# Units claimed for the first round of the weight stream, routing by logits in all groups, and a first gathering in four parts

## The chip, the cores and the metric

The kernel runs on one core of one Trainium2 chip. The metric is device time in microseconds (us), the median of repeated runs. One execution is recorded by the hardware profiler: its span runs from its first to its last instruction, and its own time is a little longer.

## The reference, cut to what matters

A two-layer block of three branches (state-space scan, sliding window, forgetting attention) is followed by a second block of three branches and a mixture of experts. The change lies in the mixture alone:

```python
t = h.reshape(-1, d)                                  # 256 tokens of 1024, after an rms norm
g_prob = softmax(t @ w_group + b_group)               # 4 groups
g_idx, g_gate = argmax(g_prob), max(g_prob)
e_logits = (t @ w_expert).reshape(-1, 4, 8) + b_expert
e_prob = softmax(e_logits[the token's group])         # 8 experts of that group
top_p, top_i = top_k(e_prob, 2)
top_w = g_gate * top_p / sum(top_p)
for e in range(32):
    hid = silu(t @ w_gate[e]) * (t @ w_up[e])         # 1024 -> 512
    out = out + combine[:, e] * (hid @ w_down[e])     # 512 -> 1024
x = x + out
```

All 32 experts' weights are read, in float32: 3 x 2 MiB each, 201 MB in all.

## The kernel before, in words

**Stages.** Two layers of the first block, then the second block (its last step is the product with `w_out_2`, line 1299), then the mixture, `moe` (from line 1385). Instructions are put in order ahead of time by a scheduler that works by priority with a model of the time; each engine then runs its own list in order. `high_priority` moves instructions forward; `pin` keeps TensorE's products of the mixture in the order in which they are written. A tile gets its buffer when its first writer is scheduled, and gives it back after its last reader.

**The weight stream.** The experts' weights come as 384 pieces of 512 KB (128 x 1024 float32), 24 for each of 16 pairs of experts: 16 pieces of `w_gate_2` and `w_up_2`, then 8 of `w_down_2`. `fetch` (line 1329) issues them on the queue of SyncE (SP) strictly in order of use, and `ring` (line 1313) says into which buffer. `RING` names 35 buffers: 2 `we`, 6 `u`, 4 `wx`, 5 `wraw`, 5 `whi`, 4 `wlo`, 4 `Thi`, 4 `Tlo` and 1 `rowb`. `FIRST` adds 4 more `u` once, so that pieces 35 to 38 (counted from 0) go into extra buffers; from piece 39 on the 35 buffers come round again, each as soon as its old piece has been read. Eight pieces are fetched inside the second block (`ahead`), the others when the buffers of the earlier stages come free.

**Units.** A `unit` (line 270) is one of 16 buffers of 128 x 1024 float32, all named `u`. In the mixture 6 of them belong to the ring, 4 hold x split into two halves (`hk`, `hlk`), 2 the router's weights (until the router's products are done), 2 each round's gathered tokens (`xg`), and 2 each pair's output (`yh`, `yl`) until it is scattered back. In the kernel before, the 4 extra units of `FIRST` are taken when their transfer is scheduled, from what is free then. `unit(True)` claims one at its place in the program by a one-column memset on GpSimd (POOL).

**Router (lines 1410 to 1497).** x is turned by TensorE (`tsplit`), ScalarE (ACT) and VectorE (DVE) write the two halves; ACT also squares x and copies it into `hk`, DVE subtracts into `hlk` (lines 1417 to 1420). Products give the logits, which are turned back (line 1437, tile `tp`) and scaled (line 1439). DVE then takes the first maximum over the groups, picks the logits of the token's group, takes the softmax with ACT, takes two first maxima of 8, and spreads the result over 32 experts (`m32`). Two products give each token's place in its expert's list (`rank`), from which `onehot` makes the matrix of a round of 4 experts.

**Rounds.** A round is 4 experts, 64 places each, in two pairs. `gather` (line 1507) brings tokens to their places, 2 of 8 slices of x at a time: 8 products and an eviction by DVE. `places` turns the one-hot matrix and gathers the weights. `hidden` does the 64 products of a pair with `w_gate_2` and `w_up_2` in 4 parts, `turned` turns the result, `down` does the 32 products with `w_down_2`, and `scatter` adds the outputs of two pairs to x. For the first round all four gathers and `places` come ahead of the first `hidden`; for later ones they stand around `turned`.

Of the kernel before, what the change touches and what calls it, by code (L numbers as in the profile page):

```python
# [25 lines left out]
F32 = mybir.dt.float32  # L26
# [16 lines left out]

FIRST = "u" * 4

# [76 lines left out]
def tile_model(ctx: ExitStack, tc: tile.TileContext, I: dict, out: bass.AP):  # L122
# [15 lines left out]
    def wtile(shape, dt, name, bufs=2):  # L138
        return (scope[0] if name in common else scope[-1]).tile(shape, dt, name=name, bufs=bufs)
# [1161 lines left out]

    extra, turns, last, fetched, slots = [], [0], [], [], []
    flat = lambda w: w.rearrange("p a n -> p (a n)")
# [48 lines left out]

    def first_max(v, n, wts, oh, mx, dst=None):

        V.tensor_reduce(mx, v, axis=AX.X, op=OP.max)
        V.tensor_tensor(oh, v, mx[:, :, None].to_broadcast([128, 2, n]), op=OP.is_equal)
        V.tensor_tensor(oh, oh, wts[:, None, :n].to_broadcast([128, 2, n]), op=OP.mult)
        cm = wtile([128, 2], F32, name="fm_c")
        V.tensor_reduce(cm, oh, axis=AX.X, op=OP.max)
        V.tensor_tensor(oh if dst is None else dst, oh, cm[:, :, None].to_broadcast([128, 2, n]), op=OP.is_equal)  # L1360

# [23 lines left out]
    def moe(router):  # L1385
# [24 lines left out]
        with tc.high_priority(HPR):  # L1410

            for c in range(2):
                for t in range(2):
                    cs = slice(512 * c, 512 * c + 512)
                    tsplit(x[:, t, cs], t, pair[c])
                    sq = wtile([128, 512], F32, name="th")
                    S.activation(sq, x[:, t, cs], AF.Square, accum_out=ss[:, t, c:c + 1])
                    xv, ps_ = x[:, t, cs].rearrange("q (p k) -> q k p", k=8), slice(64 * c, 64 * c + 64)
                    S.copy(hk[t][:, :, ps_], xv)
                    V.tensor_sub(hlk[t][:, :, ps_], xv, hk[t][:, :, ps_].bitcast(F32))  # L1420
            ps = psum.tile([128, 512], F32, name="proj", bufs=3)
            for K in range(8):
# [4 lines left out]
                if K < 7:  # L1427
                    mm(ps[0:36, :256], wrs[:, K, 0:36], xl[:, K % 4, :], False, False)
            lgT = wtile([128, 256], F32, name="lgT", bufs=1)
            S.copy(lgT[0:72], ps[0:72, :256])  # L1430
# [3 lines left out]
            tp = psum.tile([128, 4, 128], F32, name="tp", bufs=2)  # L1434
            lg = wtile([128, 2, 36], F32, name="lg", bufs=1)
            for t in range(2):
# [3 lines left out]
            mx, gate, m0, m1, z = (wtile([128, 2], F32, name=f"r{i}", bufs=1) for i in range(5))  # L1440
            ohg, t4 = R_(4, "ohg"), R_(4, "t4")
            first_max(lg[:, :, 0:4], 4, wts, ohg, mx)
            V.tensor_tensor(t4, lg[:, :, 0:4], b_(mx, 4), op=OP.subtract)
            S.activation(t4, t4, AF.Exp)
            V.tensor_reduce(gate, t4, axis=AX.X, op=OP.add)
            V.reciprocal(gate, gate)
            t32, el, pe, oh0, oh1 = R_(32, "t32"), R_(8, "el"), R_(8, "pe"), R_(8, "oh0"), R_(8, "oh1")
            for t in range(2):
                V.tensor_tensor(t32[:, t].rearrange("p (g e) -> p g e", g=4),
                                lg[:, t, 4:36].rearrange("p (g e) -> p g e", g=4),  # L1450
                                ohg[:, t, :, None].to_broadcast([128, 4, 8]), op=OP.mult)
                V.tensor_reduce(el[:, t], t32[:, t].rearrange("p (g e) -> p e g", g=4), axis=AX.X, op=OP.add)
            V.tensor_reduce(mx, el, axis=AX.X, op=OP.max)
            V.tensor_tensor(pe, el, b_(mx, 8), op=OP.subtract)
            S.activation(pe, pe, AF.Exp)
            V.tensor_reduce(z, pe, axis=AX.X, op=OP.add)
            V.reciprocal(z, z)
            V.tensor_tensor(pe, pe, b_(z, 8), op=OP.mult)
# [4 lines left out]
            member = R_(8, "member")  # L1463
            V.tensor_add(member, oh0, oh1)
            m32 = wtile([128, 2, 32], F32R, name="m32", bufs=1)

            c3 = wtile([128, 2, 16, 3], F32, name="c3", bufs=1)
            comb = c3[:, :, :, 0:2]
            for t in range(2):
                V.tensor_copy(c3[:, t, :, 2:3], rs[:, t:t + 1, None].to_broadcast([128, 16, 1]))  # L1470

            def spread(dst, src):
                for t in range(2):
                    V.tensor_tensor(dst[:, t].rearrange("p (g q) c -> p g q c", g=4),
                                    ohg[:, t, :, None, None].to_broadcast([128, 4, 4, 2]),
                                    src[:, t].rearrange("p (q c) -> p q c", c=2)[:, None].to_broadcast([128, 4, 4, 2]),
                                    op=OP.mult)
# [5 lines left out]
            pcv = pc[:, 0:128].rearrange("p (a e) -> p a e", a=4)  # L1483
            rank, many = R_(32, "rank"), R_(32, "many")
# [4 lines left out]
            V.tensor_add(z, m0, m1)  # L1489
            V.reciprocal(z, z)  # L1490
            V.tensor_mul(z, z, gate)
            V.tensor_mul(m0, m0, z)
            V.tensor_mul(m1, m1, z)
            V.tensor_tensor(oh0, oh0, b_(m0, 8), op=OP.mult)
            V.tensor_tensor(oh1, oh1, b_(m1, 8), op=OP.mult)
            V.tensor_add(oh0, oh0, oh1)
            spread(comb, oh0)

# [19 lines left out]
        def places(q, ohv, xg):  # L1518

            got = []  # L1520
            for a in range(2):
# [14 lines left out]
                got.append((xg, 128 * a, cg, ohT))  # L1536
            return got

        halves64 = (slice(0, CAP), slice(CAP, 2 * CAP))

        def hidden(p, xg, a, cg):
            pg, pu = (psum.tile([128, 512], F32, name="proj", bufs=3) for _ in range(2))
            for i in range(4):
                for ps, nme in ((pg, "w_gate_2"), (pu, "w_up_2")):
                    ws = [piece(nme, 2 * p + a, i) for a in range(2)]
                    for j in range(2):
                        k = 2 * i + j
                        for w, r in zip(ws, halves64):
                            xk = xg[k][0][:, xg[k][1], a + r.start:a + r.stop]
                            pin(T.matmul(ps[r], xk, w[:, 512 * j:512 * j + 512], start=k == 0, stop=k == 7))  # L1550
            hid = wtile([128, 512], F32, name="th")
# [43 lines left out]
        xg, ohv = [], onehot(0)  # L1595
        for k0 in range(0, 8, 2):
            gather(ohv, xg, k0)
        blocks = lambda got: [([(g[0][k // 4], k % 4) for k in range(8)], *g[1:]) for g in got]
        ready, back = blocks(places(0, ohv, xg)), []
        for p in range(16):  # L1600
            own, a, cg, ohT = ready.pop(0)
            more = not ready and p < 15
# [14 lines left out]
            if more:  # L1617
                ready = places(p // 2 + 1, ohv, xg)
                gather(ohv, xg, 4)
                gather(ohv, xg, 6)  # L1620
                ready = blocks(ready)
            back.append((down(p, hT), ohT))
# [111 lines left out]
```

## Time and profile before

| what | us |
|---|---|
| median of 3 runs | 1823.84 |
| lowest and highest run | 1822.07, 1827.51 |
| the profiled execution, its own time | 1828.07 |
| its span | 1826.3 |
| busy in the span: TensorE products / VectorE / ScalarE / GpSimd | 1711.4 / 1029.5 / 708.7 / 316.9 |
| bytes moved | 389.65 MB |

The profile cuts the span into 40 slices of about 45.7 us. In it PE is TensorE's products, PEld its weight loads, DVE VectorE, ACT ScalarE, POOL GpSimd, SP SyncE, whose queue issues the transfers. The last ten slices and a few more are the mixture; there the row of GB/s stands at 409 nearly throughout, and the slice ahead of them has 89.

### The profile page before, as it was taken

How to read it: one execution, taken by the hardware profiler on the slowest of the kernel's cores; microseconds unless marked ns; L12 is line 12 of the kernel's file. 1: busy time of each engine (PE TensorE's matmuls, PEld its weight loads, DVE VectorE, ACT ScalarE, POOL GpSimd, SP SyncE). 2: the span in 40 equal slices, each digit the busy share in tenths (PEclk: the TensorE clock that was granted, in tenths of full speed). 3: DMA queues.
4: the chain of work that ended last, by engine and by line, in shares of the span. 5: the costliest groups of instructions: out<-in, count | busy, mean ns of one | idle time of the engine just before them, and what ended most of it. 6: DMA issues, size and time to landing. Idle time of an engine off the chain costs nothing.

```text
span 1826.3 us, 24145 instructions
## 1 busy us (share of the span) xinstructions
PE 1711.4 (94%) x9005; PEld 1270.2 (70%) x9005; DVE 1029.5 (56%) x1670; ACT 708.7 (39%) x1345; POOL 316.9 (17%) x243
## 2 busy tenths in 40 slices
PE   7999999999999999999998988867799999999998
PEld 6999888888798898888877767755544343434342
DVE  6656657656664486766769998898512121211121
ACT  5556555645444656655546542413310000000000
POOL 1111116110102002311034433463000000000000
PEclk9999999999999999999999998888899999999999
DMA  8645444465466443453755532126729999999997
GB/s 268 197 132 151 133 152 129 137 196 166 145 184 192 133 143 112 133 179 106 239 165 150 152 104 71 48 91 208 252 89 406 409 409 409 409 409 409 409 409 299
DMA packets 186104, 389.65 MB, mean 213 GB/s; under 512 B 28736, under 2 KB 66816, under 8 KB 185984
## 3 DMA queue, kind: packets, MB, share of 16 engines
q1 hardware_dynamic: 185984, 388.08, 62.4%
q8 instruction: 72, 1.18, 0.3%
q14 instruction: 48, 0.39, 0.1%
HBM read 386.98 MB, written 1.05 MB: 212 GB/s over the span
## 4 chain that ended last, share of the span: by engine, by line
PE 62%; DMA 23%; DVE 10%; POOL 2%; issue 2%; ACT 1%; SPq 0%; DVEq 0%; POOLq 0%; ACTq 0%
PE proj L149 46%; PE sc L149 5%; PE pv L149 4%; DMA u<-in_w_up_dram 3%; DMA wraw<-in_w_up_dram 2%; DMA Tlo<-in_w_up_dram 2%; DMA whi<-in_w_up_dram 2%; PE proj L1550 2%; DMA wlo<-in_w_up_dram 2%; DMA Thi<-in_w_up_dram 2%; DMA wx<-in_w_up_dram 2%; DVE wlo L217 2%; PE tp L365 1%; PE sc L1571 1%; DMA wlo<-in_w_down_dram 1%
## 5 line engine op out<-in xcount | busy, mean ns | idle before, releaser
L216 ACT CAST whi<-wraw 128x1024 fp32r<-128x1024 f32 x336 | 351.8, 1051 | 316.9 <-PE proj L149 269.3
L217 DVE TENSOR_TENSOR wlo<-wraw,whi 128x1024 fp32r<-128x1024 f32 (+1 forms) x287 | 374.9, 1309 | 172.1 <-PE proj L149 121.8
L149 PE MATMUL proj<-wlo,Thi 128*128 128x512 f32 (+1 forms) x1056 | 419.4, 397 | 4.7 <-DVE wlo L217 4.6
L149 PE MATMUL proj<-whi,Thi 128*128 128x512 f32 (+1 forms) x1056 | 419.3, 399 | 2.4 <-ACT P L988 1.0
L149 PE MATMUL proj<-whi,Tlo 128*128 128x512 f32 (+1 forms) x1056 | 415.9, 396 | 0.1
L149 PEld LDWEIGHTS proj<-wlo,Thi 128*128 128x128 f32 x1056 | 201.3, 191 | 46.9 <-DVE wlo L217 6.3
L149 PEld LDWEIGHTS proj<-whi,Thi 128*128 128x128 f32 x1056 | 201.5, 191 | 44.8 <-DVE u L1273 1.9
L149 PEld LDWEIGHTS proj<-whi,Tlo 128*128 128x128 f32 x1056 | 201.0, 190 | 41.0 <-DVE Tlo L288 0.7
L217 POOL TENSOR_TENSOR wlo<-wraw,whi 128x1024 fp32r<-128x1024 f32 (+1 forms) x49 | 125.0, 2552 | 440.1 <-PE proj L149 332.9
L149 PE MATMUL proj<-Thi,wlo 128*128 128x256 f32 x576 | 165.3, 289 | 3.7 <-DVE wlo L217 3.7
L149 PE MATMUL proj<-Thi,whi 128*128 128x256 f32 x576 | 164.3, 290 | 2.9 <-ACT Thi L958 1.9
L149 PE MATMUL proj<-Tlo,whi 128*128 128x256 f32 x576 | 164.1, 289 | 0.0
L1553 DVE SCALAR_TENSOR_TENSOR th<-th,cg,proj 128x512 f32<-128x512 f32 x16 | 12.0, 747 | 267.5 <-PE proj L1550 267.5
L149 PEld LDWEIGHTS proj<-Thi,wlo 128*128 128x128 f32 x576 | 112.8, 196 | 4.1 <-DVE wlo L217 3.9
L149 PEld LDWEIGHTS proj<-Thi,whi 128*128 128x128 f32 x576 | 111.8, 195 | 4.5 <-ACT Thi L958 2.4
L149 PE MATMUL sc<-u 128*128 128x256 f32 (+1 forms) x416 | 101.1, 360 | 14.4 <-DVE u L930 14.4
L149 PEld LDWEIGHTS proj<-Tlo,whi 128*128 128x128 f32 x576 | 112.0, 196 | 0.3 <-DVE Tlo L959 0.2
L1552 ACT ACTIVATE th<-proj,cg 128x512 f32<-128x512 f32 x16 | 11.0, 687 | 234.5 <-PE proj L1550 234.5
L149 PEld LDWEIGHTS sc<-u 128*128 128x128 f32 x416 | 70.2, 197 | 22.4 <-issue 14.5
L1575 DVE TENSOR_TENSOR u<-sc,u 128x512 fp32r<-128x512 f32 x32 | 22.1, 692 | 99.8 <-ACT u L1574 99.6
L356 ACT ACTIVATE P<-sc,nm 128x256 f32<-128x256 f32 (+1 forms) x152 | 63.9, 433 | 35.9 <-DVE nm L349 21.8
L1574 ACT CAST u<-sc 128x512 fp32r<-128x512 f32 x32 | 18.8, 586 | 129.2 <-PE sc L1571 129.2
(471 smaller groups left out, 2514.4 us busy)
## 6 DMA issues: line engine op xcount, KB each, us to landing
wraw<-in_w_in_dram SPq DMA_DIRECT2D x236, 512.0 KB, 3.8
wraw<-in_w_proj_dram SPq DMA_DIRECT2D x48, 512.0 KB, 4.2
u<-in_w_up_dram SPq DMA_DIRECT2D x25, 512.0 KB, 10.2
wraw<-in_w_out_dram SPq DMA_DIRECT2D x24, 512.0 KB, 4.2
u<-in_w_gate_dram SPq DMA_DIRECT2D x24, 512.0 KB, 10.2
wraw<-in_w_up_dram SPq DMA_DIRECT2D x21, 512.0 KB, 10.2
whi<-in_w_down_dram SPq DMA_DIRECT2D x21, 512.0 KB, 10.2
u<-in_w_down_dram SPq DMA_DIRECT2D x21, 512.0 KB, 10.2
```

The costliest lines, as they stand in the source:

```text
L149: T.matmul(o, l, r, start=start, stop=stop)
L216: S.copy(hi[:, :, :n], raw[:, :, :n])
L217: (G if share[0] and scount[0] % share[0] == 0 else V).tensor_sub(lo[:, :, :n], raw[:, :, :n], hi[:, :, :n].bitcast(F32))
L356: S.activation(P[:, i * nS:(i + 1) * nS], scv[:, i, :], AF.Exp, bias=nm[:, i:i + 1], accum_out=l_out[:, i:i + 1])
L365: T.transpose(tp[:, j, :], P[:, j * 128:(j + 1) * 128], ident)
L1550: pin(T.matmul(ps[r], xk, w[:, 512 * j:512 * j + 512], start=k == 0, stop=k == 7))
L1552: S.activation(hid, pg, AF.Silu, scale=cg[:, 1:2])
L1553: V.scalar_tensor_tensor(hid, hid, cg[:, 0:1], pu, op0=OP.mult, op1=OP.mult)
L1571: pin(T.matmul(po[c][r], hT[:, k, r], w[:, 512 * c:512 * c + 512], start=k == 0, stop=k == 3))
L1574: S.copy(yh[:, c], po[c])
L1575: V.tensor_sub(yl[:, c], po[c], yh[:, c].bitcast(F32))
```

## The change

Three things. (1) The four extra units are claimed by `unit(True)` after the first `onehot`, and `ring` hands them out; before, each was taken when its transfer was scheduled. (2) The first two experts are chosen among the raw logits in all four groups at once (8 sets of 8 for the two halves of the tokens), and the group's own mask is multiplied in afterwards; the exponentials and the weights are worked out after `rank` (13 instructions on DVE and 2 on ACT, among them the three copies into `c3`), and the copies into `hk` and `hlk` stand after the router's products. (3) The first round's gathering stands inside the first `hidden`: each of its four parts goes ahead of the quarter of the products that reads it, and `places` ahead of the last quarter.

```diff
-FIRST = "u" * 4
+FIRST = 4
@@ ring
-        if n < len(RING + FIRST):
-            w = kinds[(RING + FIRST)[n]]()
-            if n < len(RING):
-                slots.append(w)
+        if n < len(RING):
+            w = kinds[RING[n]]()
+            slots.append(w)
             return w
-        return slots[(n - len(FIRST)) % len(RING)]
+        if n < len(RING) + FIRST:
+            return firsts.pop(0)
+        return slots[(n - FIRST) % len(RING)]
@@ moe, router
-                    S.copy(hk[t][:, :, ps_], xv)
-                    V.tensor_sub(hlk[t][:, :, ps_], xv, hk[t][:, :, ps_].bitcast(F32))
...
             S.copy(lgT[0:72], ps[0:72, :256])
...
+            for c in range(2):
+                for t in range(2):
+                    S.copy(hk[t][:, :, ps_], xv)
+                    V.tensor_sub(hlk[t][:, :, ps_], xv, hk[t][:, :, ps_].bitcast(F32))
...
-            first_max(lg[:, :, 0:4], 4, wts, ohg, mx)
...
-            first_max(pe, 8, wts, oh0, m0)
-            V.scalar_tensor_tensor(el, oh0, -4.0, pe, op0=OP.mult, op1=OP.add)
-            first_max(el, 8, wts, oh1, m1)
+            V.tensor_copy(el, lg[:, :, 4:36])
+            first_max(by8(el), 8, wts, by8(oh0), m0)
+            V.scalar_tensor_tensor(pe, oh0, -3e38, el, op0=OP.mult, op1=OP.add)
+            first_max(by8(pe), 8, wts, by8(oh1), m1)
+            first_max(lg[:, :, 0:4], 4, wts, ohg, mg)
             V.tensor_add(member, oh0, oh1)
-            spread(m32.rearrange("p t (q c) -> p t q c", c=2), member)
+            V.tensor_tensor(by8(m32), by8(member), b8(gexp), op=OP.mult)
...
             V.tensor_tensor(rank, rank, m32.bitcast(F32), op=OP.mult)
...
@@ hidden
             for i in range(4):
+                if prior is not None:
+                    prior(i)
@@ rounds
         xg, ohv = [], onehot(0)
-        for k0 in range(0, 8, 2):
-            gather(ohv, xg, k0)
-        ready, back = blocks(places(0, ohv, xg)), []
+        firsts.extend(unit(True) for _ in range(FIRST))
+        ready, back = [(xg, 0, None)], []
+        def opening(i):
+            gather(ohv, xg, 2 * i)
+            if i == 3:
+                ready[:] = places(0, ohv, xg)
         for p in range(16):
-            hid = hidden(p, own, a, cg)
+            hid = hidden(p, ready, opening if p == 0 else None)
```

## Rows read from the trace of the kernel before

**Rows 1.** Chain that ended last, in order of time: start us, length us, what.
```profile
1331.33 13.91 PE proj L1550 x64
...
1347.56 7.09 PE sc L1571 x32
1354.64 10.32 PE proj L1550 x48
1365.36 4.84 DMA we<-in_w_up_dram
1370.22 10.60 DMA wx<-in_w_down_dram
...
1793.50 10.18 DMA whi<-in_w_up_dram
```

**Rows 2.** Stretches: length, busy by engine, granted clock, DMA share, GB/s.
```profile
1312.00:1329.00 17.00, 9.00 (x40) 8.26 (x40) 9.28 (x56) 0.79 (x3) 0.00 (x0) 0.50 1.02 410
1329.00:1331.00 2.00, 1.78 (x18) 1.69 (x16) 1.31 (x4) 0.37 (x1) 0.00 (x0) 1.00 0.47 186
1331.00:1362.00 31.00, 29.41 (x139) 10.24 (x141) 3.63 (x10) 4.10 (x6) 0.00 (x0) 1.00 0.00 1
1362.00:1372.00 10.00, 8.09 (x30) 2.26 (x26) 0.00 (x0) 0.69 (x1) 0.00 (x0) 1.00 0.75 244
1372.00:1800.00 428.00, 410.70 (x1806) 168.50 (x1806) 79.03 (x152) 38.78 (x69) 0.00 (x0) 1.00 1.03 409
```

**Rows 3.** SP's queue in order of time: start us, length, line, target and source.
```profile
1321.09 0.33 SPq L1337 DMA_DIRECT2D u<-in_w_gate_dram  x1
...
1361.55 0.33 SPq L1337 DMA_DIRECT2D u<-in_w_gate_dram  x1
...
1364.98 0.33 SPq L1337 DMA_DIRECT2D u<-in_w_up_dram  x1
```

**Rows 4.** Waits of SP's queue, 1322 to 1363: total us, times, longest.
```profile
SPq L1337 <- PE proj L1550: 33.8, 1, 33.8
```

**Rows 5.** POOL in order of time, 1264 to 1277.
```profile
1266.83 0.10 POOL L274 MEMSET u<- 128x1 f32 x1 [0.57 <-DVE cva L968]
...
1276.08 2.65 POOL L217 TENSOR_TENSOR wlo<-wraw,whi 128x1024 fp32r<-128x1024 f32 x1 [7.88 <-DMA wx<-in_w_up_dram]
```

**Rows 6.** DVE in order of time: choice of experts, one-hot matrix, eviction of a gather.
```profile
1315.54 0.16 DVE L1355 TENSOR_REDUCE r<-lg 128x2 f32<-128x8 f32 x1
...
1320.90 0.29 DVE L1474 TENSOR_TENSOR m<-ohg,member 128x32 fp32r<-128x32 f32 x2
...
1321.92 0.23 DVE L1485 COPY many<-proj 128x64 f32<-128x64 f32 x1
...
1325.32 0.69 DVE L1515 TENSOR_TENSOR u<-tp,gw 128x512 f32<-128x512 f32 x1 [1.65 <-PE tp L1514]
```

**Rows 7.** ACT in order of time, 1308 to 1311.
```profile
1308.19 1.11 ACT L1419 CAST u<-x 128x512 fp32r<-128x512 f32 x1
1309.19 1.09 ACT L287 ACTIVATE Thi<-tp 128x512 fp32r<-128x512 f32 x2
```

**Rows 8.** PE in order of time: first gathering, then a later round's work around `turned`.
```profile
1323.23 6.53 PE L1514 MATMUL tp<-oh,u 128*128 128x256 f32 x32 [1.35 <-DVE oh L1503]
...
1372.11 2.15 PE L1514 MATMUL tp<-oh,u 128*128 128x256 f32 x16
...
1378.97 0.64 PE L1571 MATMUL sc<-we,hT 128*64 128x512 f32 x1
...
1404.76 0.50 PE L1585 MATMUL pv<-u,ohT 128*128 128x512 f32 x1
...
1409.16 0.64 PE L1571 MATMUL sc<-wlo,hT 128*64 128x512 f32 x1
```

**Rows 9.** Stretches around the first products, for the granted clock (third number from the end).
```profile
1323.00:1328.00 5.00, 4.77 (x22) 4.80 (x23) 2.02 (x6) 0.00 (x0) 0.00 (x0) 0.50 1.03 408
...
1330.00:1344.00 14.00, 13.78 (x69) 5.29 (x71) 2.19 (x9) 2.48 (x4) 0.00 (x0) 1.00 0.01 6
```

More of the change, by code (lines that the diff above doesn't have):

```diff
@@ L1299, in block2 @@
                      lambda t, ps: V.tensor_add(x[:, t, cs_], x[:, t, cs_], ps))
-    extra, turns, last, fetched, slots = [], [0], [], [], []
+    extra, turns, last, fetched, slots, firsts = [], [0], [], [], [], []
     flat = lambda w: w.rearrange("p a n -> p (a n)")
@@ L1351, in piece, with first_max @@
         return w
-    def first_max(v, n, wts, oh, mx, dst=None):
+    def first_max(v, n, wts, oh, mx):
+        r = v.shape[1]
         V.tensor_reduce(mx, v, axis=AX.X, op=OP.max)
-        V.tensor_tensor(oh, v, mx[:, :, None].to_broadcast([128, 2, n]), op=OP.is_equal)
-        V.tensor_tensor(oh, oh, wts[:, None, :n].to_broadcast([128, 2, n]), op=OP.mult)
-        cm = wtile([128, 2], F32, name="fm_c")
+        V.tensor_tensor(oh, v, mx[:, :, None].to_broadcast([128, r, n]), op=OP.is_equal)
+        V.tensor_tensor(oh, oh, wts[:, None, :n].to_broadcast([128, r, n]), op=OP.mult)
+        cm = wtile([128, 8], F32, name="fm_c")[:, :r]
         V.tensor_reduce(cm, oh, axis=AX.X, op=OP.max)
-        V.tensor_tensor(oh if dst is None else dst, oh, cm[:, :, None].to_broadcast([128, 2, n]), op=OP.is_equal)
+        V.tensor_tensor(oh, oh, cm[:, :, None].to_broadcast([128, r, n]), op=OP.is_equal)
     def runit(claim=False):
@@ L1428, in moe @@
                     mm(ps[0:36, :256], wrs[:, K, 0:36], xl[:, K % 4, :], False, False)
-            lgT = wtile([128, 256], F32, name="lgT", bufs=1)
+            lgT = wtile([128, 512], F32, name="th")[:, 0:256]
             S.copy(lgT[0:72], ps[0:72, :256])
@@ L1435, in moe @@
             lg = wtile([128, 2, 36], F32, name="lg", bufs=1)
+            for c in range(2):
+                for t in range(2):
+                    cs = slice(512 * c, 512 * c + 512)
+                    xv, ps_ = x[:, t, cs].rearrange("q (p k) -> q k p", k=8), slice(64 * c, 64 * c + 64)
+                    S.copy(hk[t][:, :, ps_], xv)
+                    V.tensor_sub(hlk[t][:, :, ps_], xv, hk[t][:, :, ps_].bitcast(F32))
             for t in range(2):
@@ L1439, in moe @@
                 V.scalar_tensor_tensor(lg[:, t], tp[:, t, 0:36], rs[:, t:t + 1], rb, op0=OP.mult, op1=OP.add)
-            mx, gate, m0, m1, z = (wtile([128, 2], F32, name=f"r{i}", bufs=1) for i in range(5))
+            small = lambda n: wtile([128, 8], F32, name=n, bufs=1)
+            m0, m1, z = (small(f"r{i}") for i in range(3))
+            mg, gate = (wtile([128, 2], F32, name=f"g{i}", bufs=1) for i in range(2))
             ohg, t4 = R_(4, "ohg"), R_(4, "t4")
-            first_max(lg[:, :, 0:4], 4, wts, ohg, mx)
@@ L1443, in moe @@
[L1443 to L1458, printed above, removed]
-            first_max(pe, 8, wts, oh0, m0)
-            V.scalar_tensor_tensor(el, oh0, -4.0, pe, op0=OP.mult, op1=OP.add)
-            first_max(el, 8, wts, oh1, m1)
-            member = R_(8, "member")
+            el, pe, oh0, oh1, member = (R_(32, n) for n in ("el", "pe", "oh0", "oh1", "member"))
@@ L1464, in moe @@
+            by8 = lambda v: v.rearrange("p t (g e) -> p (t g) e", g=4)
+            b8 = lambda v: v[:, :, None].to_broadcast([128, 8, 8])
+            V.tensor_copy(el, lg[:, :, 4:36])
[3 more added lines that the diff above has]
+            first_max(lg[:, :, 0:4], 4, wts, ohg, mg)
             V.tensor_add(member, oh0, oh1)
+            gexp = ohg.rearrange("p t g -> p (t g)")
@@ L1465, in moe @@
             m32 = wtile([128, 2, 32], F32R, name="m32", bufs=1)
[L1467 to L1477, printed above, removed]
@@ L1483, in moe @@
             pcv = pc[:, 0:128].rearrange("p (a e) -> p a e", a=4)
+            c3 = wtile([128, 2, 16, 3], F32, name="c3", bufs=1)
+            comb = c3[:, :, :, 0:2]
             rank, many = R_(32, "rank"), R_(32, "many")
@@ L1488, in moe @@
             V.tensor_tensor(rank, rank, m32.bitcast(F32), op=OP.mult)
-            V.tensor_add(z, m0, m1)
-            V.reciprocal(z, z)
[L1491 to L1497, printed above, removed]
+            V.tensor_tensor(t4, lg[:, :, 0:4], b_(mg, 4), op=OP.subtract)
+            S.activation(t4, t4, AF.Exp)
+            V.tensor_tensor(by8(el), by8(el), b8(m0), op=OP.subtract)
+            S.activation(el, el, AF.Exp)
+            V.tensor_reduce(gate, t4, axis=AX.X, op=OP.add)
+            V.reciprocal(gate, gate)
+            V.tensor_mul(member, el, member)
+            V.tensor_reduce(z, by8(member), axis=AX.X, op=OP.add)
+            V.reciprocal(z, z)
+            V.tensor_mul(z, z, gexp)
+            V.tensor_tensor(z.rearrange("p (t g) -> p t g", t=2), z.rearrange("p (t g) -> p t g", t=2), b_(gate, 4),
+                            op=OP.mult)
+            V.tensor_tensor(by8(member), by8(member), b8(z), op=OP.mult)
+            V.tensor_copy(comb, member.rearrange("p t (q c) -> p t q c", c=2))
+            for t in range(2):
+                V.tensor_copy(c3[:, t, :, 2:3], rs[:, t:t + 1, None].to_broadcast([128, 16, 1]))
+        ohTs = []
         def onehot(q):
@@ L1535, in places, with hidden @@
                     V.tensor_tensor(cg[js, 0:1], tp[js, 2, j:j + 1], cg[js, 1:2], op=OP.mult)
-                got.append((xg, 128 * a, cg, ohT))
+                got.append((xg, 128 * a, cg))
+                ohTs.append(ohT)
             return got
         halves64 = (slice(0, CAP), slice(CAP, 2 * CAP))
-        def hidden(p, xg, a, cg):
+        def hidden(p, got, prior=None):
             pg, pu = (psum.tile([128, 512], F32, name="proj", bufs=3) for _ in range(2))
             for i in range(4):
+                if prior is not None:
+                    prior(i)
+                xg, a = got[0][:2]
                 for ps, nme in ((pg, "w_gate_2"), (pu, "w_up_2")):
@@ L1548, in hidden @@
                         for w, r in zip(ws, halves64):
-                            xk = xg[k][0][:, xg[k][1], a + r.start:a + r.stop]
+                            xk = xg[k // 4][:, k % 4, a + r.start:a + r.stop]
                             pin(T.matmul(ps[r], xk, w[:, 512 * j:512 * j + 512], start=k == 0, stop=k == 7))
+            cg = got.pop(0)[2]
             hid = wtile([128, 512], F32, name="th")
@@ L1595, in moe @@
         xg, ohv = [], onehot(0)
-        for k0 in range(0, 8, 2):
-            gather(ohv, xg, k0)
-        blocks = lambda got: [([(g[0][k // 4], k % 4) for k in range(8)], *g[1:]) for g in got]
-        ready, back = blocks(places(0, ohv, xg)), []
+        firsts.extend(unit(True) for _ in range(FIRST))
[4 more added lines that the diff above has]
+                ready[:] = places(0, ohv, xg)
         for p in range(16):
-            own, a, cg, ohT = ready.pop(0)
-            more = not ready and p < 15
+            more = len(ready) == 1 and 0 < p < 15
             if more:
                 xg, ohv = [], onehot(p // 2 + 1)
-            hid = hidden(p, own, a, cg)
+            hid = hidden(p, ready, opening if p == 0 else None)
+            ohT = ohTs.pop(0)
             put = back if p % 2 == 0 or p == 15 else []
@@ L1620, in moe @@
                 gather(ohv, xg, 6)
-                ready = blocks(ready)
             back.append((down(p, hT), ohT))
```

1 line of the change is left out of this document (removed).

## The prediction

> **What bounds the kernel now.** I read the row of GB/s first. It shows that from some 1370 us to the end the kernel is one transfer after another, and that the slice ahead of this is nearly empty. The chain of waits says the same: from 1370.22 to 1803.7 it goes through transfers, each released by the one eight pieces earlier; ahead of them stand products of the first two pairs of experts and one transfer, landed 4.84 us after its issue [rows 1]. The reader is to see that the engines don't matter there: TensorE is busy 410.70 of 428 us, but only as fast as pieces land, at 409 GB/s [rows 2]. A piece of 524,288 bytes so takes 1.28 us, a pair's 24 pieces 30.8 us, a round 61.5.
>
> TensorE alone needs less for a round: two times 13.91 for `hidden` and 7.09 for `down` [rows 1], 6.86 for gathering, turning and places (1372.11 to 1378.97) and 4.40 for scattering and turning (1404.76 to 1409.16) [rows 8], together 53.3 us. So the end is set by when the stream starts and whether it is ever empty.
>
> It is empty once. Up to 1329 it moves 410 GB/s, in the next 2 us 186, from 1331 to 1362 nothing, then 244 for 10 us, and 409 after that [rows 2]. Against 410 GB/s that loses 2 x (1 - 186/410) + 31 + 10 x (1 - 244/410) = 1.1 + 31.0 + 4.0 = **36.1 us**. The queue's own waits name the cause: SP issued piece 36 (the second of the extra `u`) at 1321.09 and piece 37 at 1361.55 [rows 3], having waited 33.8 us for a product of `hidden` [rows 4]. The ring's first buffers had long been read by then (the first pair's products start at 1331.33 [rows 1]), but pieces go strictly in order, and piece 37 wanted a unit: it got the one in which the first half of `xg` stood, which the second pair reads until then. Piece 38 waited until 1364.98 [rows 3].
>
> **The claim of four units.** Counting them: 6 in the ring, 4 of `hk` and `hlk`, 4 claimed, and 2 for `xg`, which can take the router's two once its products are done. That is 16 of 16, and none of the four has to wait for a product of `hidden`. So pieces 37 and 38 follow 36 at 1.28 us, and land at 1332.5: piece 36 landed at about 1329.9, since the 0.37 MB after 1329 are 0.7 of a piece [rows 2]. What is late next is piece 39, which needs the first buffer that `hidden(0)` has read.
>
> Four memsets like the one of 0.10 us [rows 5] on an idle engine cost nothing; behind them on POOL stand the memsets of `wts` and the split at 1276.08, before which POOL is idle for 7.88 us [rows 5]. If a claim waits longer than this for a unit from the second block, that split and the products behind it are late by the rest (a rival below).
>
> What this takes away: with all 16 taken, `down(0)` has no unit for `yh` and `yl` until `hidden(1)` has read the first half of `xg` and the first extra piece. Behind them on ACT and DVE stands only the activation of `hidden(1)`, which comes later anyway. The outputs are due at the first scatter, a pair later, and their accumulators at `down(1)`, 6.86 us after `hidden(1)` [rows 8]; emptying takes two casts and two subtractions, some 3 us even if each is as long as the 0.69 of an eviction [rows 6]. I take nothing; without this cover it is at most those 3 us.
>
> **Router and gathering.** They set when piece 39 may go. Before, the gathering starts at 1323.23 [rows 8].
> - Copies moved behind the router's products: a cast of 1.11 us at 1308.19 stands ahead of the evictions at 1309.19 [rows 7]; without it these come 1.0 us earlier, with its fellow ahead of the square up to 2.2; the copies now stand between `lgT` and the gathering, and if the scheduler lets one fall in front of `lgT`, 1.1 us is lost. I take 1.2 gained (-1.1 to 2.2), since it is the nearest row.
> - Choice: from 1315.54 to 1320.90 [rows 6] there are 27 dependent steps, 0.20 us each. After, there are 14 (copy, five, one, five, two) plus the group's five beside them. Steps of 64 columns cost some 0.06 more (0.23 for 128x64 against 0.16 [rows 6]): 14 x 0.26 = 3.6, a gain of 1.8. With the group's five in the row too it is 4.9 (gain 0.5), at the old pace 2.8 (gain 2.6).
> - The 13 instructions for the weights were hidden ahead of `rank`; now those that are ready go in front of the one-hot matrix by priority. Between nothing and 13 x 0.20 = 2.6; I take 0.7, about what independent ones add while dependent ones wait.
>
> Together the gathering starts 2.3 us earlier (from 3.2 later to 4.8 earlier): 1320.9.
>
> In the first `hidden`, each part is a gather of 8, an eviction of 0.69 [rows 6] with some 0.1 of signalling, which now holds up TensorE, and 16 products. At the low clock (0.50) a gather of 8 takes 6.53/4 = 1.63, at the full one 2.15/2 = 1.08 [rows 8], and 8 products take 13.91/8 = 1.74 [rows 1] at full and 3.48 at low. The granted clock stood at 0.50 (1.2 GHz) up to 1328 and at 1.00 (2.4 GHz) from 1330 on, with the gathering running since 1323.23 [rows 8, 9]; I put the rise 6 us after the start, at 1326.9. Then the first two buffers are read at 1320.9 + 1.63 + 0.8 + 3.48 = **1326.8**, part 0 ends at 1328.6, parts 1 and 2 take 5.36 each, part 3 also the 1.57 of `places` (1329.76 to 1331.33 [rows 1, 8]) with its eviction beside them: 1345.4, against 1345.24 before. The four waits eat what the router gains; TensorE is not sooner done, but its first part is sooner read.
>
> On the clock the Trainium skill speaks against this part: TensorE: Matmul & The Clock Gate, section "HAM oscillation — how this bites in real kernels", says that products in bursts, with waits for data between them, fall back to the slow clock each time. By that rule the parts would run at 1.2 GHz (rival 2 has its price), by the rows at 2.4; no row here has bursts like these at their start.
>
> **Does the stream then stay full?** Piece n lands at 1332.5 + 1.28 (n - 38). Piece 39 at 1333.8, if issued 4.84 us earlier [rows 1], by 1329.0: its buffer is free at 1326.8. Pieces 51 and 52 would land from 1349.1, their buffers are read at 1343.7, to spare 0.6. The tight place is `down(1)`: `down(0)` starts 2.3 us after `hidden(0)` (1345.24 to 1347.56 [rows 1]) and ends at 1354.8, `hidden(1)` at 1368.7, then 6.86 us of gathering, and the first buffers of `down(1)` are read at 1375.6 + 1.8 = 1377.4. With 4.84 us pieces 75 and 76 land from 1382.2, instead of 1379.9: **2.3 us** empty. For later rounds TensorE gains 8.2 us each on the stream and finds buffers read earlier.
>
> TensorE doesn't become the bound: from the end of `down(1)` at 1382.7 it needs 13 x 26.7 + 13.9 = 361 us to the last `hidden`, 1744; the last `up` piece, 336 after piece 39, lands at 1333.8 + 433.5 = 1767.3 at the pace before (1370.2 to 1803.7 [rows 1]), some 2 later with the gap. From there to the end nothing changes.
>
> **Sum.** 36.1 - 2.3 = 33.8 us less. From the profiled execution's 1828.07 that is 1794.3. It is 4.2 us slower than the median of the runs shown; taken from this median, 1823.84, it is **1790.0**. Of this the claim is all but a little; router and gathering by themselves buy only that piece 39 and those after it don't find their buffers unread.
>
> The likeliest case's own range: with the gathering at its latest (5.5 us later than I take it) 7.8 us empty, 1795.5; with no gap 1787.7, and the lowest run lay 1.8 below the median; 1785 to 1796.
>
> **Rivals.**
> 1. *The claims disturb the end of the second block* (chance 0.07). The scheduler may give POOL's claims units that this block wants, or set them in front of the split at 1276.08 [rows 5]. For it: 8 claims instead of 4 stand there, and the fourth did wait, 0.57 us [rows 5]. Against it: POOL has 7.88 us to spare. 8 us late beyond this makes 1798.
> 2. *The clock stays low through the first `hidden`* (0.05). Parts then take 1.63 + 0.8 + 6.96, four of them and `places` 39.1 us: 1360.0, 14.6 later, and `down(1)` leaves the stream empty for 16.9 instead of 2.3: 1804.6. For it: 0.50 until 1328 [rows 9], and pauses that the gathering in one piece didn't have. Against it: 1.00 from 1330 on.
> 3. *Nothing changes* (0.04): a claimed unit isn't free in time after all, and piece 37 waits for the second pair as before [rows 4]. TensorE is at that place at the same time, 1823.8.
> 4. *Slower* (0.04): the clock stays low until `down(1)`. Its 55.8 us from 1326.9 to 1382.7 become some 106 (waits for DVE and ACT don't double), so the stream is empty for 2.3 + 50 and the kernel takes 1840. It is slower from the point at which the place is 33.8 us late, that is with the clock low for 68 us after the first products; against it, 1.00 in all the stretches after 1329 [rows 2, 9], some of them with waits of `hidden` for pieces in them.
>
> **How the numbers follow.** The likeliest case has 0.80. Faster by over 0.3% (5.5 us, about what can be told from no change): it and rivals 1 and 2, 0.92; within it rival 3, 0.04; slower rival 4, 0.04. The range of 8 in 10 takes in the likeliest case's and most of rival 1, and is cut below rival 2: 1784 to 1799.
>
> **What would show it.** Right: no pause between pieces 36 and 39 on SP's queue, GB/s at 400 or more from 1330 to 1370, the last `up` piece landing some 34 us earlier, and the chain through transfers up to it. A gap in GB/s near 1380 would be the place at `down(1)`; a waiting claim on POOL before 1290 rival 1; a granted clock of 0.50 after 1330 rival 2 or 4. Wrong would be piece 37 issued after 1340, or TensorE's work instead of transfers in the chain of the last 300 us.

## The result, and the profile after

The changed kernel takes **1796.88 us** (median of 4 runs, 1795.53 to 1801.36), the kernel before beside it 1822.95 (4 runs, 1821.20 to 1827.51): ratio 0.9857 (0.9832 to 0.9883), 26.1 us faster. In a second comparison (e1 below; the record names no chip for the first) it is 1795.96 against 1828.04, ratio 0.9822 (0.9808 to 0.9835), 32.1 us. The forecast was 1790.0 (1784 to 1799) and 33.8 us less.

The page of the kernel after: the row of GB/s (40 slices of 45 us), and the shares of the chain that ended last.

```profile
GB/s 261 188 142 137 140 145 144 148 166 164 164 174 178 171 111 141 135 164 102 197 190 149 180 106 111 66 70 107 196 378 369 410 409 408 409 409 409 409 409 297
...
PE 70%; DMA 13%; DVE 11%; issue 2%; POOL 2%; ACT 1%; SPq 0%; DVEq 0%; POOLq 0%; ACTq 0%
```

The near-empty slice is gone: 196, 378, 369 and then 408 to 410. Transfers make up 13% of the span in the chain, in the kernel before 23%; the part on the prediction comes back to this. Finer, the stretches that answer to [rows 2] (length, busy by engine, granted clock, DMA share, GB/s):

```profile
1312.00:1329.00 17.00, 6.76 (x33) 5.28 (x33) 10.79 (x51) 3.78 (x9) 0.70 (x1) 0.63 0.98 364
1329.00:1336.00 7.00, 7.00 (x24) 2.52 (x24) 0.00 (x0) 0.00 (x0) 0.00 (x0) 0.67 1.03 408
1336.00:1350.00 14.00, 12.21 (x67) 5.99 (x68) 3.69 (x11) 1.57 (x3) 0.00 (x0) 1.00 1.03 409
1350.00:1365.00 15.00, 13.38 (x64) 4.64 (x62) 0.84 (x2) 1.73 (x3) 0.00 (x0) 1.00 1.00 361
1365.00:1384.00 19.00, 18.32 (x106) 9.73 (x104) 6.41 (x15) 3.09 (x6) 0.00 (x0) 1.00 1.03 413
1384.00:1395.00 11.00, 11.00 (x54) 3.76 (x52) 1.38 (x2) 1.17 (x2) 0.00 (x0) 1.00 0.90 304
...
1395.00:1778.00 383.00, 371.08 (x1709) 154.44 (x1704) 72.52 (x137) 36.77 (x65) 0.00 (x0) 1.00 1.03 409
```

The 31 empty us are gone. Two small gaps are left, 15 x (1 - 361/410) = 1.8 and 11 x (1 - 304/410) = 2.8 us, together **4.6**. (The 364 of the first row lies ahead of this: that stretch begins 4.7 us earlier in the mixture than its fellow in [rows 2], as the shift described below shows.) SP's queue (as [rows 3]: start, length, line, target and source; a group's length reaches to the issue of its last) shows both:

```profile
1323.22 0.33 SPq L1338 DMA_DIRECT2D rowb<-in_w_up_dram  x1
1324.50 0.33 SPq L1338 DMA_DIRECT2D u<-in_w_up_dram  x1
1325.78 1.61 SPq L1338 DMA_DIRECT2D u<-in_w_gate_dram  x2
1328.34 0.33 SPq L1338 DMA_DIRECT2D u<-in_w_up_dram  x1
1332.60 0.33 SPq L1338 DMA_DIRECT2D we<-in_w_up_dram  x1
...
1350.64 0.33 SPq L1338 DMA_DIRECT2D wraw<-in_w_up_dram  x1
...
1375.91 8.72 SPq L1338 DMA_DIRECT2D we<-in_w_up_dram  x2
```

The four extra pieces go at 1324.50 to 1328.34, one each 1.28 us; in [rows 3] the third waited until 1361.55. Piece 39 (`we`) goes at 1332.60, 4.26 us after piece 38, as soon as the first eight products have read its buffer (1332.57); the stream doesn't run dry for that (408 from 1329 to 1336), since earlier pieces are still on their way (those into `u` took 10.2 us from issue to landing on the median). The two later waits are for buffers that `hidden(0)` (1350.64) and `down(1)` (the second `we`, 1384.3) read.

All of the profiled execution of after is shifted by 4.7 us ahead of the mixture: the third addition of the projection's output into `x` (DVE, L1299) starts at 1309.77 there, at 1305.08 in the profile of before, and at 1304.30 in the profile of the second comparison. But for the claims on POOL, the instructions ahead of it are the same in the same order; so I count from this addition in every run. In the table, all in us: "read" is the end of the first eight products of `hidden(0)`, "end" the end of its last products, both after that addition; "empty" is the sum of (1 - GB/s / 410) x length over stretches of 2 us from 1316 to 1420 (a minus: on the mean more than 410 GB/s); "rest" runs from the addition to the end of the span.

| kernel | read | end | empty | rest | median (runs), ratio to before |
|---|---|---|---|---|---|
| before | 28.1 | 40.1 | 36.0 | 521.2 | |
| after | 22.8 | 42.6 | 4.7 | 489.8 | 1796.88, 0.9857 |
| e1 (after again) | 22.2 | 42.6 | 4.6 | 489.9 | 1795.96, 0.9822 |
| e2 (claims alone) | 26.7 | 38.7 | 2.6 | 487.9 | 1793.03, 0.9806 |
| e3 (after, no claims) | 22.2 | 42.6 | 38.5 | 523.3 | 1830.10, 1.0013 |
| e4 (one piece) | 25.7 | 37.7 | 1.2 | 485.9 | 1793.28, 0.9803 |
| e5 (before, no extra units) | 28.2 | 40.2 | 8.9 | 493.4 | 1801.08, 0.9848 |
| e6 (gathered ahead) | 22.2 | 38.3 | 2.3 | 487.2 | 1791.84, 0.9795 |
| e7 (unread products) | 19.5 | 38.7 | -0.1 | 483.0 | 1790.26, 0.9785 |

"Rest" less "empty" lies between 484.5 and 485.3 in eight rows and at 483.1 in e7's: in the eight, what the mixture takes beyond its empty time is the same within 0.8 us. Between before and after the empty time is the whole difference, 36.0 - 4.7 = 31.3 us of 521.2 - 489.8 = 31.4.

### The profile page after: what moved, and what is told of

Its sections match the earlier page's. It is cut to its first block, busy times and chain, and to the rows that moved or that the text cites. A ratio compares the mean times of both kernels' runs of the same rounds, so it can differ in the third digit from the quotient of the medians.

```text
span 1799.6 us, 24178 instructions
## 1 busy us (share of the span) xinstructions
PE 1688.6 (94%) x9005; PEld 1266.1 (70%) x9005; DVE 1025.9 (57%) x1659; ACT 708.2 (39%) x1345; POOL 318.4 (18%) x247
## 4 chain that ended last, share of the span: by engine, by line
PE 70%; DMA 13%; DVE 11%; issue 2%; POOL 2%; ACT 1%; SPq 0%; DVEq 0%; POOLq 0%; ACTq 0%
PE proj L149 45%; PE proj L1550 7%; PE sc L149 5%; PE pv L149 4%; PE sc L1572 4%; DMA whi<-in_w_up_dram 2%; DMA Tlo<-in_w_up_dram 2%; DVE wlo L217 2%; PE tp L1509 1%; PE tp L365 1%; PE tp L286 1%; DMA wlo<-in_w_up_dram 1%; DMA wx<-in_w_up_dram 1%; DMA wraw<-in_w_down_dram 1%; DVE u L935 1%
## 5 line engine op out<-in xcount | busy, mean ns | idle before, releaser
L217 DVE TENSOR_TENSOR wlo<-wraw,whi 128x1024 fp32r<-128x1024 f32 (+1 forms) x287 | 376.7, 1316 | 172.0 <-PE proj L149 119.2
## 6 DMA issues: line engine op xcount, KB each, us to landing
u<-in_w_up_dram SPq DMA_DIRECT2D x25, 512.0 KB, 10.2
u<-in_w_gate_dram SPq DMA_DIRECT2D x24, 512.0 KB, 10.2
wraw<-in_w_up_dram SPq DMA_DIRECT2D x21, 512.0 KB, 10.2
whi<-in_w_down_dram SPq DMA_DIRECT2D x21, 512.0 KB, 10.2
```

The source lines that it names most:

```text
L217: (G if share[0] and scount[0] % share[0] == 0 else V).tensor_sub(lo[:, :, :n], raw[:, :, :n], hi[:, :, :n].bitcast(F32))
```

## The experiments

e1 to e4 ran on one chip (before: 1828.04, 15 runs), e5 to e7 on another (before: 1829.37, 9 runs); each has 5 runs of its own, e3 11.

**e1: the changed kernel again**, unedited, beside the others.

> The changed kernel once more. Its first profile had the stream empty for 4.6 us and the mixture (from the start of the third subtraction-free addition into x, the third output of the product with w_out_2, to the end) 31.4 us shorter than before (489.8 against 521.2), but everything ahead of the mixture 4.7 us later than in the profile before, from a transfer in the first 75 us, with the same order of instructions. Theory (chance): the mixture again takes 489 to 491 us, and what stands ahead of it lies anywhere from 1304 to 1310 in any run of any of these kernels; the median then is 26 to 32 us below before. Rival (the change itself costs 4.7 us ahead of the mixture): 1309 to 1311 here and in every kernel with the claims, 1304 to 1306 in those without.

1795.96 (1795.07 to 1796.35), ratio 0.9822 (0.9808 to 0.9835). Its mixture agrees with the first profile to 0.1 us. The 4.7 us ahead of the mixture don't come back: the addition starts at 1304.30 here and at 1302.92 to 1306.36 in the other kernels with claims, at 1303.92 to 1305.84 in those without, so they aren't a price of the change. That the first comparison gave 26.1 us and this one 32.1 lies for the most part in the kernel before, which was 1822.95 there and 1828.04 here, while the changed kernel was 1796.88 and 1795.96. Why the kernel before was 5 us faster there, these runs don't show.

**e2: the claims alone**, in the kernel before.

```diff
-FIRST = "u" * 4
+FIRST = 4
...
+        firsts.extend(unit(True) for _ in range(FIRST))
```

> The kernel before with the four claimed units alone (old router, gathering in one piece). Theory (the stream is all): piece 39 goes when the first products of hidden have been read, some 1.74 us after 1331.3 on the clock of the profile before, lands 4.1 us late, and nothing later is late, since TensorE isn't held up by four evictions: empty for 4 us, mixture 489 us, the same time as the changed kernel within 2 us. Rival (router and parted gathering carry part of the gain): 5 us or more slower than the changed kernel, with the stream empty for 9 us or more.

1793.03 (1790.60 to 1795.38), ratio 0.9806 (0.9793 to 0.9820): the claims bring the whole gain, and 2.9 us more than the full change (1795.96, same chip; the two ranges of runs hardly touch), where the theory had the same time within 2 us. Stretches of e2:

```profile
1323.00:1324.00 1.00, 1.00 (x6) 1.00 (x6) 0.60 (x1) 0.00 (x0) 0.00 (x0) 0.50 1.02 406
1324.00:1325.00 1.00, 1.00 (x8) 1.00 (x7) 0.10 (x2) 0.00 (x0) 0.00 (x0) 0.66 1.09 422
...
1345.00:1348.00 3.00, 3.00 (x10) 0.85 (x8) 0.00 (x0) 0.00 (x0) 0.00 (x0) 0.53 1.02 412
...
1329.00:1341.00 12.00, 12.00 (x60) 4.00 (x58) 0.78 (x4) 1.47 (x2) 0.00 (x0) 1.00 0.92 318
```

The gap is another one: 12 x (1 - 318/410) = 2.7 us around 1335, because the first buffers are read only after the whole gathering. `hidden(0)` ends 3.9 us earlier than in e1, and the place at `down(1)` has no gap.

**e3: the changed kernel without the claims.**

```diff
-FIRST = 4
+FIRST = "u" * 4
...
-        firsts.extend(unit(True) for _ in range(FIRST))
```

> The changed kernel without the claims: new router and parted gathering, the extra units taken as before when their transfer is scheduled. Theory: piece 37 waits for a unit as before, until the first half of xg has been read by the second pair, and TensorE is there some 2 us later than before (hidden(0) ends 26.2 us after the gathering starts, instead of 22.0, which starts 1.9 us earlier): 0 to 4 us slower than before, 26 to 34 slower than the changed kernel. Rival (router and gathering carry a third): 5 to 10 us faster than before.

1830.10 (1828.95 to 1832.21), ratio 1.0013 (1.0004 to 1.0022): router and parted gathering alone bring nothing, and by 2.1 us less than nothing. SP's queue of e3, and its longest wait from 1318 to 1366 (us, times, longest):

```profile
1320.10 43.11 SPq L1337 DMA_DIRECT2D u<-in_w_gate_dram  x2
```
```profile
SPq L1337 <- PE proj L1549: 31.9, 1, 31.9
```

Piece 37 again waits for the second pair, 31.9 us (33.8 in [rows 4]).

**e4: claims and new router, the gathering in one piece.**

```diff
-        ready, back = [(xg, 0, None)], []
-        def opening(i): ...
+        for k0 in range(0, 8, 2):
+            gather(ohv, xg, k0)
+        ready, back = places(0, ohv, xg), []
...
-            hid = hidden(p, ready, opening if p == 0 else None)
+            hid = hidden(p, ready, None)
```

> The changed kernel with the first gathering in one piece again (claims and new router kept). Theory: piece 39 is late by 2.3 us (its buffer is read 1.9 us sooner than with the claims alone), TensorE reaches down(1) some 4 us sooner than in the changed kernel, so no second gap: empty for 2 to 3 us instead of 4.6, 2 us faster than the changed kernel. Rival (the parts are what keeps the stream full): 3 us or more slower than the changed kernel.

1793.28 (1790.24 to 1794.11), ratio 0.9803 (0.9789 to 0.9816). The same as e2 in time, so the new router is worth nothing that the runs can tell (by the table 1.4 us of empty time, 1.2 left where 2 to 3 were expected); parting the gathering costs the 2.7 us between this and e1, not the router.

**e5: the kernel before without any extra units**, a ring of 35.

```diff
-FIRST = "u" * 4
+FIRST = ""
```

> The kernel before with no extra units at all: the ring has its 35 buffers and piece 35 takes the first of them again. So far the mixture took 484.7 to 485.3 us plus the time for which the stream was empty, in six profiles of five kernels. Theory (what cost 33.8 us was that piece 37, which wanted a unit, stood in the queue ahead of pieces whose buffers were free): taking the extra units away must win most of what the claims win. Piece 35 is issued some 1.8 us after the first products start (1331.3 on the clock of the profile before), lands near 1337.5 instead of 1328.6: empty for 8 to 10 us instead of 36, mixture 493 to 496, 26 to 28 us faster than before. Rival (the four pieces fetched early are the gain, as buffers): no faster than before by more than 3 us.

1801.08 (1798.39 to 1803.16), ratio 0.9848 (0.9832 to 0.9865). SP's queue and one stretch:

```profile
1318.86 0.33 SPq L1337 DMA_DIRECT2D rowb<-in_w_up_dram  x1
1334.01 0.33 SPq L1337 DMA_DIRECT2D we<-in_w_up_dram  x1
```
```profile
1328.00:1341.00 13.00, 12.78 (x69) 6.79 (x69) 3.39 (x11) 2.03 (x3) 0.00 (x0) 0.93 0.47 142
```

Piece 35 now waits for the ring's first buffer, read at 1334.0, and the stream is empty for 13 x (1 - 142/410) = 8.5 us there. So the four extra units as the kernel before had them didn't help: they cost 28 us against none, since the third was bound to a unit that the second pair still read, and everything queued behind it. Claimed in time, they are worth some 6 us over none: 8.9 - 2.6 us of empty time (the ratios, 0.9806 against 0.9848, would make it 7.7, but come from two chips).

**e6: the changed kernel, each part gathered one quarter earlier**, so that evictions lie beside products.

```diff
-            gather(ohv, xg, 2 * i)
+            for k0 in ((0, 2), (4,), (6,), ())[i]:
+                gather(ohv, xg, k0)
```

> The changed kernel with each of the first round's gathers one part earlier: two ahead of the first quarter of the products, one each ahead of the second and third, and the places ahead of the fourth. Theory (TensorE's three waits of 0.8 us for an eviction inside the first hidden, and with them the second gap near down(1)): hidden(0) ends some 2.5 us sooner after the gathering's start than the 26.2 of the changed kernel, the stream is empty for 0.5 to 2.5 us instead of 4.6, and the mixture takes 486 to 487.5. Rival (the gap comes from the first products being late): they start 1 to 2 us later here, so it is empty for 5 to 6.5 us.

1791.84 (1788.34 to 1793.06), ratio 0.9795 (0.9778 to 0.9811). `hidden(0)` ends 4.3 us earlier than in after, and 2.4 of 4.7 us of empty time go. Two stretches of e6 suggest why not all:

```profile
1345.00:1348.00 3.00, 3.00 (x10) 0.90 (x8) 0.00 (x0) 0.00 (x0) 0.00 (x0) 0.52 1.04 411
...
1370.00:1384.00 14.00, 13.51 (x71) 6.00 (x73) 4.37 (x12) 1.66 (x4) 0.00 (x0) 1.00 0.94 338
```

The clock, 1.00 from 1324, fell in `down(0)` for some 3.5 us. `down(0)` so took 8.6 us from its first product to the next `hidden`'s, against 6.9 in after, and the place at `down(1)` has 14 x (1 - 338/410) = 2.5 us empty. That the 1.7 us are most of these 2.5 is argued from the sizes; no run has e6 without the fall.

**e7: the changed kernel with ten products that nobody reads**, so that TensorE is busy while DVE chooses the experts: seven after the router's products, three after those of the places. The output doesn't change.

```diff
+            warm = psum.tile([128, 512], F32, name="proj", bufs=3)
+            held = wtile([128, 72], F32R, name="held", bufs=1)
+            S.copy(held, lg.rearrange("p t e -> p (t e)"))
+            for _ in range(7):
+                mm(warm[0:72], held, hh[0][:, 0:512], True, True)
...
+            for _ in range(3):
+                mm(warm[0:64], m32.rearrange("p t e -> p (t e)"), hh[0][:, 0:512], True, True)
```

> The changed kernel with ten added products whose results nothing reads, seven beside DVE's choice of experts and three behind the two products for the places, so that TensorE doesn't stand still ahead of the gathering. Theory (the low clock at the start of the first hidden is the other part of the second gap): the granted clock is 1.00 before the first products instead of some 7 us after the gathering starts, hidden(0) ends 3 to 5 us sooner after that start, the stream is empty for 0.5 to 2 us instead of 4.6, the mixture takes 485.5 to 487.5. Rival (the clock there costs nothing that counts): 4 us or more empty.

1790.26 (1785.53 to 1793.61), ratio 0.9785 (0.9765 to 0.9805), the lowest median of all, though the ranges of e2, e4 and e6 overlap with its own. It never ran beside the changed kernel: its ratio lies below e1's 0.9822 (0.9808 to 0.9835), but the changed kernel's own two ratios, 0.9857 and 0.9822, lie as far apart. That it is faster rests on the times, of which its slowest (1793.61) is below the changed kernel's fastest (1795.07), and on its mixture, 6.8 us shorter. Its opening on TensorE (start, length, line, out and in, count, the wait before it):

```profile
1315.66 3.26 PE L149 MATMUL proj<-u,held 128*72 128x512 f32 x7 [0.79 <-ACT held L1448]
...
1321.10 1.22 PE L1516 MATMUL tp<-oh,u 128*128 128x256 f32 x8 [0.39 <-DVE oh L1505]
1323.10 1.94 PE L1557 MATMUL proj<-we,u 128*64 128x512 f32 x8 [0.78 <-DVE u L1517]
```
```profile
1319.00:1321.00 2.00, 1.71 (x5) 0.92 (x5) 1.79 (x13) 0.00 (x0) 0.00 (x0) 0.67 1.03 420
1321.00:1344.00 23.00, 20.33 (x108) 9.69 (x108) 5.18 (x17) 2.72 (x4) 0.00 (x0) 1.00 1.03 410
```

With the clock at 1.00 from the first gather on, the part of 8 gathers takes 1.22 us instead of 2.04 and the first eight products 1.94 instead of 3.68. From the first gather to the end of `hidden(0)` it takes 23.1 us, and the stream loses nothing. Its mixture, 483.0, is below the 485.5 to 487.5 of the theory: this version is also 1.4 to 2.2 us shorter than the others beyond its gaps. Its stream ran at 411 to 412 GB/s in the last slices instead of 409, for which I have no cause.

## Why the prediction was right, and where its size was off

**The claim: right, and the whole of the gain.** Pieces 37 and 38 followed at 1.28 us, the stream's 36.0 empty us fell to 4.7, and without the claims nothing of it is left (e3). Rival 3 is out. Rival 1 too: the four claims on POOL (start, length, line; the wait before it) are the memsets at 1274.12, 1281.10, 1283.81 and 1286.81 here, against [rows 5]:

```profile
1274.12 0.10 POOL L274 MEMSET u<- 128x1 f32 x1 [1.17 <-DVE u L1377]
1281.10 0.10 POOL L274 MEMSET u<- 128x1 f32 x1 [6.88 <-DVE u L1274]
1281.28 2.59 POOL L217 TENSOR_TENSOR wlo<-wraw,whi 128x1024 fp32r<-128x1024 f32 x1
1283.81 0.10 POOL L274 MEMSET u<- 128x1 f32 x1
1286.81 0.10 POOL L274 MEMSET u<- 128x1 f32 x1 [2.90 <-DVE u L1274]
```

One does wait 6.88 us for the second block ahead of a split, as the rival said, but that split at 1281.28 stood at 1276.08 before; less the shift of 4.7 it is 0.5 us later, and the addition behind it isn't late in e2 (1303.67) or in any other profile with claims but this one (see e1).

**Emptying `yh`, `yl`: no cost**, as taken. Their casts wait for `hidden(1)` (14.08 us, at 1368.72) and are done, with the subtractions, by 1373.5; `down(1)` starts at 1382.4.

**The choice of experts: right.** On DVE (as [rows 6]) it takes from 1320.24 to 1323.60, 3.36 us where [rows 6] show 5.36: 2.0 gained, 1.8 taken.

```profile
1320.24 0.20 DVE L1453 COPY el<-lg 128x64 f32<-128x64 f32 x1
...
1323.60 0.22 DVE L1461 TENSOR_TENSOR m<-member,ohg 128x64 fp32r<-128x64 f32 x1
```

**The moved copies: wrong, nothing gained instead of 1.2.** ACT took them in front of the evictions all the same, as in [rows 7]; it seems that the scheduler ordered them by when their data were ready, not by where they stand in the code:

```profile
1311.18 1.18 ACT L1439 CAST u<-x 128x512 fp32r<-128x512 f32 x1
...
1312.88 1.09 ACT L1439 CAST u<-x 128x512 fp32r<-128x512 f32 x1
1313.88 1.07 ACT L287 ACTIVATE Thi<-tp 128x512 fp32r<-128x512 f32 x2
```

**The weights behind the choice: smaller than taken.** From the products of the places to the first gather it was 1.99 us and is 2.19: 0.2 lost, not 0.7. The three together: the gathering starts 1.85 us earlier (18.15 us after the addition before, 16.30 now) and 2.4 in e1 (15.73), forecast 2.3. That the sum came out so near is in part luck: the 1.2 of the copies are missing, the other two were 0.2 and 0.5 better than taken, and what lies ahead of the choice varies as much from run to run, from 8.25 to 8.91 us between the addition and the products that turn the logits (8.90 before, 8.91 in after, 8.35 in e1), with either router.

**The opening: the step that was mis-sized.** From the first gather to the end of `hidden(0)` the forecast had 24.5 us. TensorE in after, in order of time (as [rows 8]), and the clock (third number from the end):

```profile
1323.88 0.42 PE L149 MATMUL proj<-m,upper 128*128 128x64 f32 x1 [4.13 <-DVE m L1461]
...
1326.07 2.04 PE L1509 MATMUL tp<-oh,u 128*128 128x256 f32 x8 [1.56 <-DVE oh L1498]
1328.89 3.68 PE L1550 MATMUL proj<-we,u 128*64 128x512 f32 x8 [0.78 <-DVE u L1510]
1332.36 2.52 PE L1550 MATMUL proj<-u 128*64 128x512 f32 x8
1334.81 1.21 PE L1509 MATMUL tp<-oh,u 128*128 128x256 f32 x8
1336.81 3.65 PE L1550 MATMUL proj<-u 128*64 128x512 f32 x16 [0.78 <-DVE u L1510]
1340.39 1.21 PE L1509 MATMUL tp<-oh,u 128*128 128x256 f32 x8
...
1345.97 1.22 PE L1509 MATMUL tp<-oh,u 128*128 128x256 f32 x8
...
1348.68 3.65 PE L1550 MATMUL proj<-wraw,u 128*64 128x512 f32 x16
```
```profile
1326.00:1329.00 3.00, 2.15 (x10) 1.89 (x12) 1.20 (x5) 0.00 (x0) 0.00 (x0) 0.50 1.03 411
1329.00:1333.00 4.00, 4.00 (x10) 1.14 (x12) 0.00 (x0) 0.00 (x0) 0.00 (x0) 0.50 1.02 407
1333.00:1334.00 1.00, 1.00 (x6) 0.38 (x4) 0.00 (x0) 0.00 (x0) 0.00 (x0) 0.68 1.05 418
1334.00:1350.00 16.00, 14.21 (x80) 6.99 (x76) 3.69 (x11) 1.57 (x3) 0.00 (x0) 1.00 1.03 409
```

It took 26.3 us, 26.9 in e1. The eviction waits came as sized (0.78 against 0.8). Three terms were too small. The first gather took 2.04 instead of 1.63, and with its eviction it held TensorE up for 0.4 more: the 6.53 from which the forecast took its price at the low clock end at 1329.76 [rows 8], and the clock had risen by then, at some 1328.8 (0.79 on the mean from 1328 to 1330). The clock rose 7.6 us after the gather's start (1333.6; 8.8 in e1: 0.57 in the us from 1328, 1.00 from 1329), not 6, which makes the second eight products 0.7 longer (2.45 us to the next gather instead of 1.74). And the other three parts took 5.58, 5.58 and 6.36 instead of 5.36, 5.36 and 6.13, together 0.7 more. That is the 1.8. With the gathering 0.5 us later in after, `hidden(0)` so ended 42.6 us after the addition instead of the forecast 40.3 (1345.4 less 1305.08): 2.3 us more. From there on every duration was as taken: 2.32 to `down(0)`, 7.09, 13.73, 6.89 to `down(1)`. So all of the 2.3 went to the stream. The transfers at `hidden(0)`'s last buffers, which had 0.6 to spare, lost 1.8, and the place at `down(1)` has the rest, 2.8: 2.3 + 2.3 = 4.6 empty. The forecast of a gap at that place, and of its size given the end of `hidden(0)`, was right. Rivals 2 and 4 are out: the clock stayed at 1.00 from 1334 to the end of the stream.

That products in bursts fall back to 1.2 GHz each time, as the Trainium skill has it (TensorE: Matmul & The Clock Gate, section "HAM oscillation — how this bites in real kernels"), doesn't show here: after the rise the clock stayed at 1.00 through two eviction waits of 0.78 us. The waits of that section's example are 3 to 5 us, so the prediction took from it more than it says of waits like these.

What the bursts did here is another thing: they came at the low clock and left it late, 7.6, 8.8 and 8.8 us after the first gather in after, e1 and e3. Where 32 gathers came in a row, it rose 3.4 us after the first of them in e2 (0.66 in the us from 1324), and 5.6, 5.8 and 6.1 us after it in before, e4 and e5. One row of e4 and one of e5, where the first gather starts at 1321.99 and at 1323.83:

```profile
1327.00:1329.00 2.00, 2.00 (x17) 2.00 (x15) 1.07 (x2) 0.00 (x0) 0.00 (x0) 0.82 1.02 408
...
1328.00:1330.00 2.00, 2.00 (x12) 2.00 (x11) 0.98 (x2) 0.00 (x0) 0.00 (x0) 0.53 0.10 35
```

So bursts are later in all three profiles than products in a row in all four. Why e2's rise came so early these runs don't show.

**The chain: in part not as forecast.** A sign of being right was to be the chain through transfers up to the last `up` piece, as in [rows 1]. In after it goes through TensorE's products until 1540, and through transfers only then (with products again from 1653.85 to 1674.64):

```profile
1533.87 2.10 PE tp L1509 x16
...
1540.60 10.15 DMA whi<-in_w_up_dram
...
1767.83 10.18 DMA whi<-in_w_up_dram
```

With the 31 us gone, TensorE comes out of the opening behind the stream, and pieces wait for the buffers that it reads. It catches up, since a round takes it 52.8 us (from `hidden(2)` at 1389.43 to `hidden(4)` at 1442.20) against the stream's 61.5, much as forecast. The time is the stream's all the same: from 1395 to 1778 it moved 409 GB/s without a gap. The last `up` piece landed at 1778.0, 468.2 us after the addition, where it was 498.6 before: 30.4 earlier, forecast some 34.

**The sum.** 31.4 us within the mixture instead of 33.8. The 2.3 are the opening. e7 changes the clock of that opening and little else (its gathering starts 15.6 us after the addition, against 16.3 and 15.7 in after and e1); none of the 4.7 empty us are left there, so with the clock up the opening is in time for the stream. In e6, which has no eviction waits there, half of them are left. The forecast of the time itself, 1790.0, was 6.9 too low, and the opening is only a third of this. It took the 33.8 from the median of the kernel before, 1823.84, and this kernel was 1828.04 and 1829.37 on the two chips of the experiments; from the profiled execution, 1828.07, it would have been 1794.3. The 26.1 us of the first comparison fall short of 31.4 for the most part for the same reason. The statement that router and parted gathering buy only an earlier read of the first buffers held (22.2 against 28.1), but this wasn't what bound any more: with the claims, parting the gathering moved the gap from around 1335 (e2, e4) to `down(1)` and made it larger.

## What to carry to other kernels

In a queue that issues in order, a further buffer helps only if it is free when its turn comes; one that waits blocks all that follow, and fewer buffers may be faster (e5 against before). Count the units at the point of their use, and claim them where they come free. When a stream is the bound, list the places where it can run dry with the time that each has to spare: work put earlier for one of them (the parted gathering) can be paid at the next, and its worth is the change of the largest lateness, not of one.

## What was not expected of the hardware

- Ten products whose result nobody reads took the stream's empty time from 4.7 us to none, since TensorE left 1.2 GHz before the work that the stream waits for. The kernel was some 0.4% faster than with the change alone (ratios 0.9785 and 0.9822, on two chips), of which the stream's higher rate, for which no cause was found, is probably a part.
- The clock fell back to about half in `down(0)` in e2 (0.53 from 1345 to 1348) and e6 (0.52), though it had been 1.00 for some 20 us, and TensorE had only paused for 0.95 and 0.68 us around the activation of `hidden(0)`. The seven other profiles have the same two pauses (0.92 to 0.95 and 0.67 to 0.68) and no fall. What decides it these runs don't show.
- One core drew 409 GB/s for 383 us on end, in pieces of 0.52 MB, and 411 to 412 in e7.
